# The last layer norm of a hybrid encoder layer: from three engines with a hand-set lag to VectorE and ScalarE alone

## The chip, the cores and the metric

One core of one Trainium2 chip runs the whole layer as one program. The metric is device time in microseconds (us) of that core, from runs that compute the reference's output. The engines are named as in the profile: PE is TensorE, DVE is VectorE, ACT is ScalarE, POOL is GpSimd, SP is SyncE, which here only issues transfers.

## The reference, cut to what matters

The layer takes 2048 tokens of width 1024: a projection, a gated delta rule in both directions beside attention, an output product, a first norm, a mixture of 32 experts (two per token), and a last norm. Only the end matters here:

```python
x = layer_norm(ALPHA * x + gt1 * mixed, ln1_g, ln1_b)
h = layer_norm(x) * (1.0 + sc2) + sh2
ffn = hierarchical_moe(h, ...)
x = layer_norm(ALPHA * x + gt2 * ffn, ln2_g, ln2_b)   # the last norm

def layer_norm(x, gain, bias):
    mu = mean(x); var = mean(square(x - mu))           # over the 1024 columns
    return (x - mu) * rsqrt(var + 1e-5) * gain + bias
```

## The kernel before

**Stages.** `run` (L2127) calls the stages in order: projections, attention, recurrence, output product with the first norm (`mix`), experts (`experts`, L2050) and the last norm (`tail`, L2078). Tokens are tiled in 16 tiles of 128 rows (one row per partition) by 1024 columns in 32-bit floats, 512 KB each.

**What comes before the last norm.** The scaled residual stream lies in device memory in `d_x1`. The experts work through blocks of 128 token slots and, between them, three "quads" (four small experts at once; `quads`, L1968, puts their steps at fixed places among the blocks). Each block and each quad ends with an indirect transfer issued by POOL that adds its rows into `d_x1` (L1893, L1964). The loads of the last norm read `d_x1`, so they wait for the last of these additions. Gain and bias, `g2` and `b2`, are loaded to all partitions at the end of `experts` (L2067, L2068) into tiles that held gathered tokens (they are called `xg` in the profile).

**The last norm.** `tail` first issues 16 loads from SP's queue, one tile each (L2085). Then three steps per tile are written out by hand with lags: in round t, `stats` of tile t, `scale` of tile t - 2 and `shift` of tile t - 5 (`SL`, `TL`, L2122 to L2125). Inside `manual_schedule` the engines named take their instructions in the order in which they are written.

- `stats` (L2091): for 13 tiles DVE takes the moments, two `bn_stats` of 512 columns and one `bn_aggr` (`ln_moments`, L221 and L222), and ACT takes the square root (L2101). For tiles 4, 8 and 12 (`TA`) ACT makes the moments itself: a pass whose sum goes to a column of `mv` (L2094), two small instructions that divide it (L2095, L2096), a pass that squares the centred tile and sums it (L2097), and the square root (L2098). A pass with a sum is two instructions in the profile, the pass and a read of the accumulator.
- `scale` (L2103): DVE inverts the root (L2105) and forms -mean/deviation in a column of `mv` (L2111); ACT makes the normalised tile in one pass (L2112); POOL multiplies it by `g2` (L2113). The last tile (`TP` = 1) takes another way: DVE does it in two passes, (y - mean) * g2 and y / deviation + b2 (L2107, L2108).
- `shift` (L2115): DVE adds `b2` (L2117) and ACT's queue issues the store of the tile (L2118; L2109 for the last tile).

The first norms, in `mix_norm`, use the same two DVE passes on tiles of the same size (L1330, L1333) with a reciprocal between them (L1331).

Of the kernel before, what the change touches and what calls it, by code (L numbers as in the profile page):

```python
# [13 lines left out]
AF = mybir.ActivationFunctionType  # L14
OP = mybir.AluOpType
# [4 lines left out]
D = 1024  # L20
S = 2048
NT = S // 128
# [9 lines left out]
ET = mybir.EngineType  # L32
# [14 lines left out]
FEW, QS = 32, 3  # L47
QA = (13, 18, 21, 24, 27, 30, 33, 36, 39)
QL = ((0, 1), (2, 3))
TP, SL, TL = 1, 2, 5  # L50
TA = (4, 8, 12)


def dram_ap(t, offset, ap):
# [3 lines left out]
class Layer:  # L58
# [2019 lines left out]
    def tail(self):  # L2078
        nc, tc, A = self.nc, self.tc, self.A
        with self.pool("tail", 1) as wp:  # L2080
            row = lambda t: slice(t * 128, t * 128 + 128)
            Y = [wp.tile([128, D], F32, name=f"y{t}") for t in range(NT)]
            g2, b2 = self.g2, self.b2
            for t in range(NT):
                nc.sync.dma_start(Y[t], self.d_x1[row(t)])  # L2085

            mv = [wp.tile([128, 3], F32, name=f"mv{t}") for t in range(NT)]

            sq = wp.tile([128, D], F32, name="sq")

            def stats(t):  # L2091
                y, m, act = Y[t], mv[t], nc.scalar.activation
                if t in TA:
                    act(sq, y, AF.Identity, accum_out=m[:, 2:3])  # L2094
                    act(m[:, 0:1], m[:, 2:3], AF.Identity, scale=1.0 / D)  # L2095
                    act(m[:, 2:3], m[:, 2:3], AF.Identity, scale=-1.0 / D)  # L2096
                    act(sq, y, AF.Square, bias=m[:, 2:3], accum_out=m[:, 1:2])  # L2097
                    act(m[:, 1:2], m[:, 1:2], AF.Sqrt, bias=self.eps[1e-5], scale=1.0 / D)  # L2098
                    return
                self.ln_moments(wp, y, m)  # L2100
                act(m[:, 1:2], m[:, 1:2], AF.Sqrt, bias=self.eps[1e-5])  # L2101

            def scale(t):  # L2103
                y, m = Y[t], mv[t]
                nc.vector.reciprocal(m[:, 1:2], m[:, 1:2])  # L2105
                if t >= NT - TP:
                    nc.vector.scalar_tensor_tensor(y, y, m[:, 0:1], g2, op0=OP.subtract, op1=OP.mult)  # L2107
                    nc.vector.scalar_tensor_tensor(y, y, m[:, 1:2], b2, op0=OP.mult, op1=OP.add)  # L2108
                    nc.scalar.dma_start(A["out"][0, row(t), :], y)  # L2109
                    return  # L2110
                nc.vector.scalar_tensor_tensor(m[:, 2:3], m[:, 0:1], -1.0, m[:, 1:2], op0=OP.mult, op1=OP.mult)  # L2111
                nc.scalar.activation(y, y, AF.Identity, bias=m[:, 2:3], scale=m[:, 1:2])  # L2112
                nc.gpsimd.tensor_tensor(y, y, g2, op=OP.mult)  # L2113

            def shift(t):  # L2115
                if t < NT - TP:
                    nc.vector.tensor_tensor(Y[t], Y[t], b2, op=OP.add)  # L2117
                    nc.scalar.dma_start(A["out"][0, row(t), :], Y[t])  # L2118

            with tc.manual_schedule(engines={ET.DVE, ET.Activation, ET.Pool}):  # L2120
                nc.scalar.activation(mv[0][:, 2:3], self.eps[1e-5], AF.Sqrt)
                for t in range(NT + TL):  # L2122
                    for f, lag in ((stats, 0), (scale, SL), (shift, TL)):
                        if 0 <= t - lag < NT:
                            f(t - lag)  # L2125

    def run(self):  # L2127
        tc = self.tc
# [66 lines left out]
```

## Time and profile before

| | us |
|---|---|
| median of 3 runs | 2256.69 |
| lowest and highest run | 2247.44, 2260.79 |
| the profiled execution, its own time | 2251.07 |
| its span, first to last instruction | 2249.3 |

Share of the span in which each engine is busy: PE 90%, DVE 73%, ACT 56%, POOL 39%. These are averages over all stages; the last norm takes the final 3% of the span, from the first load at 2180.1 us to the end at 2249.3 us, and PE does nothing there. Times in rows are us from the span's start, durations in the columns "mean" or "min/median/max" are ns. A row of the timeline gives start, duration, engine, line, operation, output<-input and count; a duration includes time in which the instruction was held back after it had started, and the starts of neighbours can be closer than their durations, since the end of one overlaps the beginning of the next.

### The profile page before, as it was taken

The numbers are of one execution on the slowest core, as the hardware profiler recorded it, in microseconds if no ns is written. First come the engines' busy times: TensorE is split into PE (matmuls) and PEld (weight loads), VectorE is DVE, ScalarE is ACT, GpSimd is POOL, SyncE is SP. The second block draws the span as 40 slices with busy tenths as digits, with TensorE's granted clock in tenths as the row PEclk, the third lists the DMA queues.
The fourth block names the chain that finished last, engine by engine and source line by source line (L and its number), as shares of the span: only waits on it lengthen the run. The fifth ranks groups of instructions, "written<-read, shape, count | busy, mean of one in ns | idle before, by whom it ended". The sixth has DMA issues, their size and how long they took to land. (4 is left out here: it accounts for less than half of the span.)

```text
span 2249.3 us, 43324 instructions
## 1 busy us (share of the span) xinstructions
PE 2024.6 (90%) x15381; PEld 1784.8 (79%) x15381; DVE 1650.0 (73%) x3412; ACT 1253.9 (56%) x3049; POOL 882.7 (39%) x940
## 2 busy tenths in 40 slices
PE   6999998999999999989899999999996999999940
PEld 4899997999998888878888898888775777676630
DVE  5787748288775888878787556799776877676649
ACT  4776755367754778767777444334333555454424
POOL 0311134311131447686866455402244343333227
PEclk8999999999999999999999999999997999999975
DMA  7445653445445774677752788654534999999955
GB/s 275 147 125 152 152 175 109 125 130 148 138 138 140 223 192 131 171 185 175 202 113 62 270 289 294 221 178 169 144 113 138 271 324 320 330 323 337 326 174 216
DMA packets 406939, 441.34 MB, mean 196 GB/s; under 512 B 79947, under 2 KB 331179, under 8 KB 405691
## 3 DMA queue, kind: packets, MB, share of 16 engines
q1 hardware_dynamic: 388187, 394.30, 57.1%
q0 software_dynamic: 13920, 33.71, 6.1%
q10 hardware_dynamic: 4608, 10.49, 1.2%
q8 instruction: 123, 2.02, 0.4%
q14 instruction: 101, 0.83, 0.1%
HBM read 352.15 MB, written 121.37 MB: 211 GB/s over the span
## 5 line engine op out<-in xcount | busy, mean ns | idle before, releaser
L73 PE MATMUL pj<-wh,hthi 128*128 128x256 f32 (+1 forms) x768 | 225.5, 294 | 3.1 <-DVE lnmv L222 3.1
L74 PE MATMUL pj<-wl,hthi 128*128 128x256 f32 (+1 forms) x768 | 220.0, 286 | 2.8 <-DVE wl L68 2.8
L73 PE MATMUL pj<-hthi,wh 128*128 128x260 f32 x768 | 222.5, 290 | 0.0
L75 PE MATMUL pj<-wh,htlo 128*128 128x256 f32 (+1 forms) x768 | 220.1, 287 | 1.4 <-DVE htlo L275 1.4
L207 POOL TENSOR_TENSOR xa<-xa 128x512 f32<-128x512 f32 (+2 forms) x96 | 84.2, 877 | 349.0 <-ACT xa L205 304.7
L68 DVE TENSOR_TENSOR ptl<-pt,pth 128x512 fp32r<-128x512 f32 x256 | 176.1, 688 | 58.9 <-ACT pth L67 57.6
L75 PE MATMUL pj<-hthi,wl 128*128 128x260 f32 x768 | 217.1, 283 | 0.0
L74 PE MATMUL pj<-htlo,wh 128*128 128x260 f32 x768 | 216.6, 282 | 0.0
L67 ACT CAST pth<-pt 128x512 fp32r<-128x512 f32 x256 | 150.3, 587 | 96.9 <-PE pt L884 94.0
L329 DVE SCALAR_TENSOR_TENSOR cacc<-pj,convw,cacc 128x256 f32<-128x256 f32 x384 | 183.9, 481 | 10.0
L875 ACT ACTIVATE p<-s,mx 128x512 f32<-128x512 f32 x256 | 176.9, 691 | 14.7 <-DVE mx L866 12.9
L863 DVE TENSOR_REDUCE mx<-s 128x1 f32<-128x512 f32 x256 | 175.1, 684 | 9.6 <-PE s L75 4.0
L1893 POOL DMA_INDIRECT d_x<-ye,tid x40 | 76.3, 1908 | 257.4 <-DMA d_x<-ye,tid 118.2
L73 PE MATMUL o<-pth,vh 128*128 128x256 f32 x512 | 166.0, 324 | 0.2 <-ACT oT L904 0.2
L884 PEld LDWEIGHTS pt<-ident,p 128*128 128x128 f32 x1024 | 125.3, 141 | 44.6 <-DVE ptl L68 14.2
L884 PE MATMUL pt<-ident,p 128*128 128x128 f32 x1024 | 156.2, 275 | 3.7 <-DVE ptl L68 3.3
L68 DVE TENSOR_TENSOR w13l<-raw,w13h 128x2048 fp32r<-128x2048 f32 x54 | 123.6, 2290 | 39.1 <-ACT w13h L67 38.1
L73 PEld LDWEIGHTS pj<-wh,hthi 128*128 128x128 f32 x768 | 148.1, 193 | 3.3 <-issue 3.3
L74 PEld LDWEIGHTS pj<-wl,hthi 128*128 128x128 f32 x768 | 148.0, 193 | 3.0 <-DVE wl L68 3.0
L75 PEld LDWEIGHTS pj<-wh,htlo 128*128 128x128 f32 x768 | 147.9, 193 | 2.1 <-DVE htlo L275 2.1
L75 PE MATMUL o<-pth,vl 128*128 128x256 f32 x512 | 144.9, 283 | 0.0
L74 PEld LDWEIGHTS pj<-htlo,wh 128*128 128x128 f32 x768 | 144.8, 189 | 0.0
(534 smaller groups left out, 6369.4 us busy)
## 6 DMA issues: line engine op xcount, KB each, us to landing
raw<-in_w_dram SPq DMA_DIRECT2D x116, 512.0 KB
raw<-in_w_dram SPq DMA_DIRECT2D x29, 1024.0 KB
sh<-d_sh SPq DMA_DIRECT2D x32, 768.0 KB
qraw<-in_w_dram SPq DMA_DIRECT2D x48, 512.0 KB
xa<-in_w_ada_dram SPq DMA_DIRECT2D x32, 512.0 KB
dr<-d_dir SPq DMA_DIRECT2D x32, 512.0 KB
wraw<-in_w_in_dram SPq DMA_DIRECT2D x96, 128.0 KB
qraw<-in_w_dram SPq DMA_DIRECT2D x12, 1024.0 KB
```

The lines of the kernel that those rows point to most:

```text
L67: (copy or self.nc.scalar.copy)(hi, src)
L68: (engine or self.nc.vector).tensor_tensor(lo, src, hi, op=OP.subtract)
L73: mm(out, a[0], b[0], start=start, stop=False)
L74: mm(out, a[0], b[1], start=False, stop=False)
L75: mm(out, a[1], b[0], start=False, stop=stop)
L207: nc.gpsimd.tensor_tensor(w[:, :n], w[:, :n], w[:, n:2 * n], op=OP.add)
L329: nc.vector.scalar_tensor_tensor(acc, ps[:, j:j + BLK], self.convw[:, j, ct:ct + 1], acc, op0=OP.mult, op1=OP.add)
L863: nc.vector.tensor_reduce(mx[:, i:i + 1], ps, axis=AX.X, op=OP.max)
L875: self.nc.scalar.activation(p[:, i * 512:i * 512 + 512], ps[i], AF.Exp, bias=mx[:, 4:5], scale=scale, accum_out=sm[:, i:i + 1])
L884: nc.tensor.transpose(pt[:, i, t], self.P[u, t][0][:, (2 * g + i) * 128:(2 * g + i + 1) * 128], self.ident)
L1893: self.nc.gpsimd.indirect_dma_start(out=self.d_x1, out_offset=bass.IndirectOffsetOnAxis(ap=self.tid[:, self.col(i)], axis=0), in_=self.YE. ...
```

## The change

The moments of 14 tiles are made by ACT in two summing passes (the scale of the first makes its sum the negative mean at once, so that the small divisions go); tiles 0 and 2 (`TD`) keep DVE's `bn_stats`. These two are written ahead of the loop. Every tile is then finished by DVE in the two passes that only the last tile took before. POOL has no work left in the stage, the lags are gone, and the stores are issued by SP's queue, behind the loads, instead of ACT's. Nothing else in the program is changed.

```diff
--- before.py
+++ after.py
@@ -47,8 +47,7 @@
 FEW, QS = 32, 3
 QA = (13, 18, 21, 24, 27, 30, 33, 36, 39)
 QL = ((0, 1), (2, 3))
-TP, SL, TL = 1, 2, 5
-TA = (4, 8, 12)
+TD = (0, 2)
 
 
 def dram_ap(t, offset, ap):
@@ -2085,44 +2084,32 @@
                 nc.sync.dma_start(Y[t], self.d_x1[row(t)])
 
             mv = [wp.tile([128, 3], F32, name=f"mv{t}") for t in range(NT)]
-
             sq = wp.tile([128, D], F32, name="sq")
 
-            def stats(t):
+            def moments(t):
+
                 y, m, act = Y[t], mv[t], nc.scalar.activation
-                if t in TA:
-                    act(sq, y, AF.Identity, accum_out=m[:, 2:3])
-                    act(m[:, 0:1], m[:, 2:3], AF.Identity, scale=1.0 / D)
-                    act(m[:, 2:3], m[:, 2:3], AF.Identity, scale=-1.0 / D)
-                    act(sq, y, AF.Square, bias=m[:, 2:3], accum_out=m[:, 1:2])
-                    act(m[:, 1:2], m[:, 1:2], AF.Sqrt, bias=self.eps[1e-5], scale=1.0 / D)
+                if t in TD:
+                    act(m[:, 1:2], m[:, 1:2], AF.Sqrt, bias=self.eps[1e-5])
                     return
-                self.ln_moments(wp, y, m)
-                act(m[:, 1:2], m[:, 1:2], AF.Sqrt, bias=self.eps[1e-5])
-
-            def scale(t):
+                act(sq, y, AF.Identity, scale=-1.0 / D, accum_out=m[:, 0:1])
+                act(sq, y, AF.Square, bias=m[:, 0:1], accum_out=m[:, 1:2])
+                act(m[:, 1:2], m[:, 1:2], AF.Sqrt, bias=self.eps[1e-5], scale=1.0 / D)
+
+            def finish(t):
                 y, m = Y[t], mv[t]
+                nc.vector.scalar_tensor_tensor(y, y, m[:, 0:1], g2, op0=OP.subtract if t in TD else OP.add, op1=OP.mult)
                 nc.vector.reciprocal(m[:, 1:2], m[:, 1:2])
-                if t >= NT - TP:
-                    nc.vector.scalar_tensor_tensor(y, y, m[:, 0:1], g2, op0=OP.subtract, op1=OP.mult)
-                    nc.vector.scalar_tensor_tensor(y, y, m[:, 1:2], b2, op0=OP.mult, op1=OP.add)
-                    nc.scalar.dma_start(A["out"][0, row(t), :], y)
-                    return
-                nc.vector.scalar_tensor_tensor(m[:, 2:3], m[:, 0:1], -1.0, m[:, 1:2], op0=OP.mult, op1=OP.mult)
-                nc.scalar.activation(y, y, AF.Identity, bias=m[:, 2:3], scale=m[:, 1:2])
-                nc.gpsimd.tensor_tensor(y, y, g2, op=OP.mult)
-
-            def shift(t):
-                if t < NT - TP:
-                    nc.vector.tensor_tensor(Y[t], Y[t], b2, op=OP.add)
-                    nc.scalar.dma_start(A["out"][0, row(t), :], Y[t])
-
-            with tc.manual_schedule(engines={ET.DVE, ET.Activation, ET.Pool}):
+                nc.vector.scalar_tensor_tensor(y, y, m[:, 1:2], b2, op0=OP.mult, op1=OP.add)
+                nc.sync.dma_start(A["out"][0, row(t), :], y)
+
+            with tc.manual_schedule(engines={ET.DVE, ET.Activation}):
                 nc.scalar.activation(mv[0][:, 2:3], self.eps[1e-5], AF.Sqrt)
-                for t in range(NT + TL):
-                    for f, lag in ((stats, 0), (scale, SL), (shift, TL)):
-                        if 0 <= t - lag < NT:
-                            f(t - lag)
+                for t in TD:
+                    self.ln_moments(wp, Y[t], mv[t])
+                for t in range(NT):
+                    moments(t)
+                    finish(t)
 
     def run(self):
         tc = self.tc
```

## Rows read from the trace of the kernel before

**Rows 1.** The chain of waits that ended last: start, us, what.
```profile
2180.14 3.50 DMA y<-d_x
...
2185.42 1.30 DVE lnst L221 x2
...
2186.99 1.30 DVE lnst L221 x2
...
2213.14 0.72 DVE mv L2111
2213.86 1.14 DVE y L2117
2214.99 1.21 DVE lnst L221 x2
...
2242.82 2.27 DVE y L2117 x2
```

**Rows 2.** Busy us by stretch: instructions (x), PE clock, DMA share, GB/s.
```profile
2184.00:2190.00 6.00, 0.00 (x0) 0.00 (x0) 5.66 (x14) 2.04 (x4) 0.00 (x0) 0.50 1.02 410
...
2190.20:2240.60 50.40, 0.00 (x0) 0.00 (x0) 49.58 (x70) 28.82 (x45) 47.14 (x15) 0.50 0.55 222
...
2227.10:2227.60 0.50, 0.00 (x0) 0.00 (x0) 0.50 (x2) 0.28 (x1) 0.50 (x2) 0.50 0.21 82
...
2247.00:2248.00 1.00, 0.00 (x0) 0.00 (x0) 0.00 (x0) 0.00 (x0) 0.00 (x0) 0.50 0.72 287
```

**Rows 3.** Instructions on tile y: count, duration ns min/median/max, first and last start.
```profile
L2113 POOL TENSOR_TENSOR y<-y,xg x15: 2340/3393/3399, 2190.1 to 2237.3; 128x1024 f32<-128x1024 f32 x15
L2117 DVE TENSOR_TENSOR y<-y,xg x15: 1210/1211/1212, 2196.1 to 2243.9; 128x1024 f32<-128x1024 f32 x15
...
L2107 DVE SCALAR_TENSOR_TENSOR y<-y,mv,xg x1: 3283/3283/3283, 2235.1 to 2235.1; 128x1024 f32<-128x1024 f32 x1
```

**Rows 4.** Groups of instructions, end of the span: count, busy us, mean ns, idle before.
```profile
L2111 DVE SCALAR_TENSOR_TENSOR mv<-mv 128x1 f32<-128x1 f32 x15 | 17.5, 1166 | 0.5
```

**Rows 5.** Timeline: DVE's reciprocal and the small product after it, tile 0.
```profile
2188.43 0.11 DVE L2105 RECIPROCAL mv<-mv 128x1 f32<-128x1 f32 x1
...
2188.58 0.16 DVE L2111 SCALAR_TENSOR_TENSOR mv<-mv 128x1 f32<-128x1 f32 x1
```

**Rows 6.** The first norms' DVE passes, by line, columns as in rows 3.
```profile
L1330 DVE SCALAR_TENSOR_TENSOR raw<-raw,lnmv,g x16: 1265/1284/1473, 1459.0 to 1678.5; 128x1024 f32<-128x1024 f32 x16
...
L1333 DVE SCALAR_TENSOR_TENSOR xg<-xg,lnmv,sh x16: 1272/1277/1281, 1466.1 to 1684.3; 128x1024 f32<-128x1024 f32 x16
```

**Rows 7.** Timeline: such a pass and the reciprocal behind it.
```profile
1678.54 1.27 DVE L1330 SCALAR_TENSOR_TENSOR raw<-raw,lnmv,g 128x1024 f32<-128x1024 f32 x1
1679.74 0.15 DVE L1331 RECIPROCAL lnmv<-lnmv 128x1 f32<-128x1 f32 x1
```

**Rows 8.** Timeline: ACT's own moments of tile 4.
```profile
2193.66 1.04 ACT L2094 ACTIVATE sq<-y 128x1024 f32<-128x1024 f32 x1
...
2194.82 0.20 ACT L2095 ACTIVATE mv<-mv 128x1 f32<-128x1 f32 x1
...
2195.29 1.15 ACT L2097 ACTIVATE sq<-y,mv 128x1024 f32<-128x1024 f32 x1
...
2196.56 0.29 ACT L2098 ACTIVATE mv<-mv,eps 128x1 f32<-128x1 f32 x1
2196.76 1.23 ACT L2112 ACTIVATE y<-y,mv 128x1024 f32<-128x1024 f32 x1
```

**Rows 9.** SP's queue: its loads and what they waited for (us, times, longest).
```profile
2180.14 17.34 SPq L2085 DMA_DIRECT2D y<-d_x  x16
...
SPq L2085 <- DMA y<-d_x: 10.5, 7, 2.2
```

**Rows 10.** Timeline: the issue of one store, late in the stage.
```profile
2225.10 0.34 ACTq L2118 DMA_DIRECT2D out_dram<-y  x1
```

**Rows 11.** The page's groups: a DVE operation of twice the columns.
```profile
L68 DVE TENSOR_TENSOR w13l<-raw,w13h 128x2048 fp32r<-128x2048 f32 x54 | 123.6, 2290 | 39.1 <-ACT w13h L67 38.1
```

## The prediction

> **What bounds the kernel now.** I read the chain of waits from its end, since the change touches only the last norm. From the first load at 2180.14 to the end it has no PE work: one load (3.50 us), then DVE without a break until 2245.09 (2242.82 + 2.27), then the last store [rows 1]. DVE is on the chain, but is DVE full of work? The stretch table says no more than that it never idles: 49.58 of 50.40 us, with POOL at 47.14 [rows 2]. The groups settle it. L2111 works on one column per partition, took 0.16 us before POOL had started [rows 5], and averages 1166 ns over its 15 cases [rows 4]: 17.5 us of DVE's time, of which some 15 us (15 x 1.0) are no work. POOL's multiply takes 2340 ns at its quickest and 3393 ns in the median; the difference, 1.05 us, is near the 1.21 us of DVE's addition L2117 [rows 3]. So in this trace the two engines hold each other back wherever both work on tensors or columns of this stage, and a tile costs their sum. The reader should see the rhythm in the chain: held small product 0.72, addition 1.14, `bn_stats` 1.21 [rows 1], 3.07 us, which with the aggregate and the reciprocal fill up the 3.39 us of POOL's multiply [rows 3]. The bound is POOL's multiply plus what DVE does in POOL's gaps; the loads are in by about 2203 (worked out below) and ACT has 28.82 of 50.40 us to do [rows 2].
>
> **The change part by part.** Everything is counted in the span's time, from the moment at which DVE can begin to finish tiles.
>
> *Start.* The load order and the wait before it are unchanged, so tile 0 is seen at 2183.64 [rows 1]. At 410 GB/s [rows 2] a tile of 0.524 MB takes 1.28 us, so tile 2 is there at 2186.2 and the last at 2202.8 (estimates; the trace shows that its statistics could start at 2186.99, the upper end, and 2185.42, where tile 1's started, is the lower end). One tile's statistics take 1.57 us (2185.42 to 2186.99) [rows 1]. DVE has tile 0's done before; it begins tile 0's first pass at 2186.2 + 1.57 = 2187.8, between 2187.0 and 2188.6.
>
> *DVE per tile.* Two passes of 1024 columns and a reciprocal. The operation is the one of L1330 and L1333, same shape and memory: 1284 and 1277 ns in the median [rows 6]; since ends overlap, the next instruction starts 1.20 us after (1678.54 to 1679.74) [rows 7]. The reciprocal with the instruction that needs it costs 0.15 (2188.43 to 2188.58) [rows 5]. That makes 1.20 + 0.15 + 1.20 = 2.55 us, 16 times 40.8 us. Ends: 0.07 less if the second pass started during the reciprocal, 0.05 more if each wait on ACT costs an instruction: 2.48 to 2.60, that is 39.7 to 41.6. Held at the slowest pass seen, 1.473 [rows 6], a tile would take 2.93 and all 46.9. I take 2.55, because the two medians differ by 7 ns and only one form has such an outlier.
>
> *ACT per tile.* First summing pass 1.16 (2193.66 to 2194.82, accumulator read included), second 1.27 (2195.29 to 2196.56), root 0.20 [rows 8]: 2.63 us; the two small divisions between them (0.47) go. With nothing saved it would be the whole 3.10 (2193.66 to 2196.76). ACT begins tile 1 when it has taken tile 0's root, at about 2185.7, ends it at 2188.3, takes tile 2's root and does 13 more tiles by 2188.6 + 34.2 = 2222.8. DVE wants the last tile's sums at 2187.8 + 15 x 2.55 = 2226.1. So ACT's passes are hidden, with 3.3 us to spare; it would become the bound above about 2.88 us a tile. ACT waits for DVE only at tiles 0 and 2; nothing else is queued behind those waits that could be run earlier.
>
> *What goes.* POOL's 15 multiplies, ACT's 15 normalising passes, the 15 additions, the 15 small products with their stalls, and 11 of 13 tiles' `bn_stats` on DVE. Nothing is put down to these singly: they are replaced by the new pace.
>
> *The stores.* 16 issues of 0.34 us [rows 10] move from ACT's queue to SP's, behind the loads. SP issues loads for 17.34 us, to 2197.5, because from the ninth on it waits for earlier ones to land [rows 9]. So the first three stores (ready from 2190.4) wait till 2197.5, and the load data occupies the transfers until about 2202.8. This costs nothing as long as the 16 stores, 16 x 1.28 = 20.5 us of data, can follow: 2223.3 at the earliest, ahead of DVE. If a store were put ahead of a load, that load would be late by the store's wait, but harmless while at least four tiles lie between them (landing 3.5, ACT 2.6, DVE 2.55, against 2.55 per tile).
>
> *End.* DVE's last pass ends at 2187.8 + 40.8 + 0.1 (the overlap that nothing follows) = 2228.7. A lone store issued at 2225.10 [rows 10] moves its last bytes at about 2227.2 (82 of 410 GB/s in the half microsecond from 2227.1) [rows 2], 2.1 us after. From the last bytes, 2247.7 (287 of 410 in the microsecond from 2247.0) [rows 2], to the span's end are 1.6 us. Before, four stores came within 3.4 us and queued, and the end lay 4.2 us after DVE; now 3.7, between 3.5 and 4.2. The end is 2232.4.
>
> **Sum.** 2249.3 - 2232.4 = 16.9 us less (0.75%). On the profiled execution's 2251.07 that is 2234.2. This execution stands 5.6 us below the median of the runs shown; from the median, 2239.8.
>
> **A rule that speaks against it.** In the first norms a pass of this operation over 1024 columns, all from on-chip memory, takes 1.28 us [rows 6], and an addition of as many columns takes 1.21 [rows 3], so it runs nearly at the addition's rate. The Trainium skill, Vector Engine (DVE) Microarchitecture Reference, section 7 (Points that are easy to get wrong), says that this shape of instruction has half the throughput when both its sources are in SBUF and neither is bf16. By that, DVE would be slower after the change than before (second rival); these rows disagree.
>
> **Rivals.**
>
> *First: the pass is longer here, and the gain shrinks.* DVE and ACT now stream tiles while transfers run at 410 GB/s. At 1.473 us a pass the gain is 16.9 - 6.1 = 10.8 us. For: one of 16 passes of that form took it [rows 6]. Against: the medians of both lines lie within 1%, and L1333's 16 cases between 1272 and 1281 ns. ACT as the bound belongs here: at 3.10 it ends at about 2189 + 40.3, DVE 2.5 us later at 2231.8, a gain of 13.8. Chance 0.13.
>
> *Second: half rate.* A pass then costs what twice the columns cost, 2.29 us [rows 11]; a tile takes 2 x 2.29 + 0.15 = 4.7, all 75.7, the end 2187.8 + 75.7 + 3.7 = 2267.2: 18 us slower. It decides from the point at which 16 tiles fill the time to the old end: (2249.3 - 3.7 - 2187.8) / 16 = 3.61 a tile, 1.73 us a pass. Against it stand rows 6. The page named above would have it so. Chance 0.02.
>
> *Third: the pass is slow in this stage itself.* The nearest row in place is L2107, the same pass on the same tiles, and it took 3.28 us [rows 3]. If that is not POOL's doing, a tile costs 2 x 3.28 + 0.15 = 6.7 us and the end comes at 2187.8 + 107.2 + 3.7 = 2298.7, 49 us slower; the same 1.73 decides. Against: POOL's last multiply starts at 2237.3 [rows 3], and L2107 (2235.1 + 3.28 = 2238.4) ends 1.1 us after that, so it fits a pass that waited for the multiply before it. Chance 0.03.
>
> **How the numbers follow.** The forecast has the rest, 0.82. A measurement of this kernel tells some 0.5%, 11.3 us, from no change. The shown runs alone spread over 13 us, so I let the forecast's 16.9 be measured below 11.3 in one case of eight (0.10), and half of the first rival: faster 0.72 + 0.06 = 0.78, same 0.10 + 0.07 = 0.17, slower 0.05. The bounds of the terms give a gain of 10.8 to 19.1 (best tile 1.1, best start 0.8, best end 0.2 more, with a little rounding). The lowest run less the forecast gain is 2230.5, the highest less the least gain 2250.0; the range is 2230 to 2250, and leaves out the second and third rival and a part of the first.
>
> **What would show it.** Right: L2107 and L2108 sixteen times each (under the changed kernel's numbers) at 1.27 to 1.29 us, starts of one tile's first pass 2.55 apart, DVE never idle from 2187.8 to 2228.7, ACT at 2.63 a tile and finished some 3 us ahead, no POOL work, 3.7 us from DVE's end to the span's. Wrong: DVE waiting for ACT before first passes (first rival), passes at 2.3 (second) or 3.3 (third), loads issued after stores, or a stretch before 2180 that has moved by more than a few us.

## The result, and the profile after

The changed kernel took 2237.74 us in the median of four runs (2234.89 to 2242.82), the kernel before 2256.86 in the median of its four (2247.44 to 2260.79). The ratio is 0.9921, with a 95% interval of 0.9898 to 0.9944: faster by 0.8%, and by more than 0.5% over the whole interval. The profiled execution took 2234.89 us with a span of 2233.0, 16.2 us less than the profiled execution of before (2251.07), where 16.9 were forecast.

First the instructions on tile `y`, with the columns of rows 3 (count, duration in ns as min/median/max, first and last start). L2101 and L2103 are DVE's two passes, L2095 and L2096 ACT's two summing passes, L2104 the stores, L2084 the loads:

```profile
L2084 SPq DMA_DIRECT2D y<-d_x x16: 319/325/469, 2179.6 to 2192.8; - x16
L2101 DVE SCALAR_TENSOR_TENSOR y<-y,mv,xg x16: 1276/1280/1285, 2187.5 to 2226.3; 128x1024 f32<-128x1024 f32 x16
L2103 DVE SCALAR_TENSOR_TENSOR y<-y,mv,xg x16: 1283/1285/1286, 2188.9 to 2227.7; 128x1024 f32<-128x1024 f32 x16
...
L2095 ACT ACTIVATE sq<-y x14: 1039/1040/1042, 2185.2 to 2219.7; 128x1024 f32<-128x1024 f32 x14
...
L2096 ACT ACTIVATE sq<-y,mv x14: 1147/1148/1150, 2186.4 to 2220.9; 128x1024 f32<-128x1024 f32 x14
```

All 32 DVE passes lie between 1276 and 1286 ns, where the one of L2107 took 3283 before [rows 3]. POOL has no row in the stage any more, and the 3393 ns multiply and the held product of 1166 ns [rows 3, 4] are gone with it. Next, two tiles in the timeline (start, duration, engine, line; in brackets the idle time before and what ended it):

```profile
2184.78 0.21 DVE L221 BATCH_NORM_AGGREGATE mv<-lnst 128x2 f32<-128x12 f32 x1
...
2185.90 1.29 DVE L220 BATCH_NORM_STATS2 lnst<-y 128x6 f32<-128x512 f32 x2 [0.91 <-DMA y<-d_x]
...
2187.49 1.28 DVE L2101 SCALAR_TENSOR_TENSOR y<-y,mv,xg 128x1024 f32<-128x1024 f32 x1
...
2188.70 0.16 DVE L2102 RECIPROCAL mv<-mv 128x1 f32<-128x1 f32 x1
2188.89 1.28 DVE L2103 SCALAR_TENSOR_TENSOR y<-y,mv,xg 128x1024 f32<-128x1024 f32 x1
...
2190.09 1.28 DVE L2101 SCALAR_TENSOR_TENSOR y<-y,mv,xg 128x1024 f32<-128x1024 f32 x1
...
2222.18 0.29 ACT L2097 ACTIVATE mv<-mv,eps 128x1 f32<-128x1 f32 x1
...
2227.73 1.28 DVE L2103 SCALAR_TENSOR_TENSOR y<-y,mv,xg 128x1024 f32<-128x1024 f32 x1
```

DVE stands 0.91 us for tile 2's load, begins the first pass at 2187.49, and from there each tile takes 2.59 us (the next tile's first pass starts at 2190.09; the last second pass ends at 2229.01, so 16 tiles took 41.5). ACT is done at 2222.5, 3.9 us before DVE begins the last tile at 2226.34. Last, what SP's queue waited for (us in total, times, longest), which answers to rows 9:

```profile
SPq L2104 <- DVE y L2103: 25.2, 12, 2.2
SPq L2084 <- DMA y<-d_x: 6.7, 7, 1.6
SPq L2104 <- DMA y<-d_x: 4.5, 5, 0.9
```

Twelve times a store waits for DVE, at most 2.2 us: the stores are not behind. In what follows "the stage" is the time from the first load's issue to the end of DVE's last pass: 2180.14 to 2245.09 before, 64.95 us, and 2179.56 to 2229.01 after, 49.45 us. It is the measure for small edits, for a reason that the last section shows.

### The profile page after: what moved, and what is told of

The parts are those of the page before. It is cut to its first block, busy times and chain, and to the rows that moved or that the text cites. A ratio compares the mean times of both kernels' runs of the same rounds, so it can differ in the third digit from the quotient of the medians.

```text
span 2233.0 us, 43291 instructions
## 1 busy us (share of the span) xinstructions
PE 2018.3 (90%) x15381; PEld 1783.1 (80%) x15381; DVE 1632.6 (73%) x3379; ACT 1260.4 (56%) x3072; POOL 838.5 (38%) x925
## 5 line engine op out<-in xcount | busy, mean ns | idle before, releaser
L1892 POOL DMA_INDIRECT d_x<-ye,tid x40 | 81.0, 2026 | 253.5 <-DMA d_x<-ye,tid 112.2
L73 PE MATMUL o<-ptl,vh 128*128 128x256 f32 x512 | 145.0, 283 | 0.0
```

The source lines that it names most:

```text
L73: mm(out, a[0], b[1], start=False, stop=False)
L1892: self.nc.gpsimd.indirect_dma_start(out=self.d_x1, out_offset=bass.IndirectOffsetOnAxis(ap=self.tid[:, self.col(i)], axis=0), in_=self.YE. ...
```

## The experiments

All runs in one table: the median or single time in us, that of the kernel before on the same chip, and the stage. But for the run with three rounds (six runs) they are single runs.

| run | time | before beside it | stage |
|---|---|---|---|
| 16 multiplications on POOL | 2268.39 | 2249.26 | 79.2 |
| 40 fills on POOL | 2243.02 | 2249.26 | 50.4 |
| 16 scalings on POOL | 2245.11 | 2257.46 | 58.1 |
| before, multiplication on DVE | 2287.2 | 2249.26 | 91.9 |
| before, multiplication on DVE, lagged | 2245.61 | 2252.61 | 63.2 |
| all moments on DVE | 2266.58 | 2252.61 | 70.2 |
| stores on ACT's queue | 2276.33 | 2249.26 | 90.9 |
| one tile's moments on DVE | 2244.64 | 2257.46 | 47.7 |
| reciprocal first | 2231.34 | 2252.61 | 49.1 |
| reciprocal first, tiles 0 and 1, last tile halved (3 rounds) | 2237.24 | 2252.61 | 48.4 |
| interleaved | 2239.41 | 2265.0 | 47.4 |
| interleaved, tiles 0 and 1 | 2239.76 | 2265.0 | 47.7 |

### Does POOL's multiply hold DVE, or was it the shared data?

```diff
-            with tc.manual_schedule(engines={ET.DVE, ET.Activation}):
+            with tc.manual_schedule(engines={ET.DVE, ET.Activation, ET.Pool}):
...
+                pw = wp.tile([128, D], F32, name="pw")
+                nc.gpsimd.tensor_copy(pw[:, 0:1], mv[0][:, 0:1])
+                for _ in range(16):
+                    nc.gpsimd.tensor_tensor(pw, b2, g2, op=OP.mult)
                 for t in range(NT):
                     moments(t)
                     finish(t)
```

> The changed kernel with 16 multiplications on POOL added (128x1024 f32, gain by bias into a tile of its own), none of which DVE or ACT waits for; they begin once tile 0's mean is there. Theory (POOL's two-input multiply and DVE's two-input pass hold each other back, whatever data they work on): each multiply takes about 3.4 us in place of 2.34, a DVE pass that meets one shows about 3.3 us in place of 1.28, and the stage, from the first load's issue to DVE's end, grows from 49.5 us by about 16 x 2.2 = 35 to some 84 us. Rival (in the kernel before it was the data, POOL and DVE working in turn on the same tile, that cost the time): the stage stays at 49.5 within 1 us and passes at 1.28.

The stage took 79.2 us (2183.41 to 2262.59), 29.7 more. DVE and POOL in the timeline, at the end of POOL's row of multiplications:

```profile
2227.76 13.04 POOL L2113 TENSOR_TENSOR pw<-xg,xg 128x1024 f32<-128x1024 f32 x4
2228.69 3.35 DVE L2101 SCALAR_TENSOR_TENSOR y<-y,mv,xg 128x1024 f32<-128x1024 f32 x1
2231.97 0.15 DVE L2102 RECIPROCAL mv<-mv 128x1 f32<-128x1 f32 x1
2232.16 3.17 DVE L2103 SCALAR_TENSOR_TENSOR y<-y,mv,xg 128x1024 f32<-128x1024 f32 x1
2235.25 3.35 DVE L2101 SCALAR_TENSOR_TENSOR y<-y,mv,xg 128x1024 f32<-128x1024 f32 x1
...
2238.71 3.17 DVE L2103 SCALAR_TENSOR_TENSOR y<-y,mv,xg 128x1024 f32<-128x1024 f32 x1
2241.80 1.27 DVE L2101 SCALAR_TENSOR_TENSOR y<-y,mv,xg 128x1024 f32<-128x1024 f32 x1
```

While POOL multiplies, each pass takes 3.2 to 3.4 us; the first pass after POOL's last one takes 1.27. Nothing of DVE's reads or waits for `pw`, so it is not two engines working in turn on one tile. The multiplications do read `b2` and `g2`, which DVE's passes read as well; that no common tile is needed is shown by the kernel before, where L2111 works on columns of `mv` alone and still averages 1166 ns beside POOL's multiply of `y` by `g2`, for 0.16 us without it [rows 4, 5]. Expected were 35. A tile takes 6.56 us here (L2101 starts at 2228.69 and 2235.25) for 2.59 in the changed kernel, and two multiplications go with it: 2.0 us for each, not 2.2, and the first of the 16 fell into `bn_stats`, which it did not hold. 15 x 2.0 = 30.

### Which POOL work holds it?

```diff
-                for _ in range(16):
-                    nc.gpsimd.tensor_tensor(pw, b2, g2, op=OP.mult)
+                for _ in range(40):
+                    nc.gpsimd.memset(pw, 0.0)
```

> The changed kernel with 40 fills of zeros on POOL added (128x1024 f32 into a tile of its own, about 0.95 us each by the trace of before), from the same point on. Theory of a hold by any POOL work: passes of DVE wait, the stage grows from 49.5 us by 20 us or more. Rival (only POOL work that reads its operands from SBUF holds DVE): passes stay at 1.28, the stage at 49.5 within 1 us.

By tile, the fills of this run, and then DVE's passes beside them:

```profile
L2113 POOL MEMSET pw<- x40: 950/951/952, 2192.7 to 2232.0; 128x1024 f32 x40
```

```profile
L2101 DVE SCALAR_TENSOR_TENSOR y<-y,mv,xg x16: 1277/1279/1285, 2195.7 to 2234.6; 128x1024 f32<-128x1024 f32 x16
```

The fills run beside all of DVE's passes but the last three, and neither side is held. The stage took 50.4 us, and the 0.95 more is tile 2's load, for which DVE stood 1.86 us here and 0.91 in the changed kernel:

```profile
2194.10 1.29 DVE L220 BATCH_NORM_STATS2 lnst<-y 128x6 f32<-128x512 f32 x2 [1.86 <-DMA y<-d_x]
```

So it is not any POOL work. The same place with 16 scalings that read one tensor:

```diff
-                    nc.gpsimd.tensor_tensor(pw, b2, g2, op=OP.mult)
+                    nc.gpsimd.tensor_scalar(pw, b2, 2.0, None, op0=OP.mult)
```

> The changed kernel with 16 one-input scalings on POOL added (128x1024 f32, twice the bias into a tile of its own), as in the run with 16 multiplications. Theory (POOL work that reads SBUF holds DVE's two-input passes, one input or two): DVE passes stretch and the stage grows by about 16 times the scaling's own duration less what overlaps, 15 us or more. Rival (two engines with two inputs each are needed): passes stay at 1.28 and the stage at 49.5 within 1 us.

Again by tile, the scalings and then DVE's passes:

```profile
L2113 POOL TENSOR_SCALAR pw<-xg x16: 2786/3088/3112, 2187.0 to 2234.3; 128x1024 f32<-128x1024 f32 x16
```

```profile
L2101 DVE SCALAR_TENSOR_TENSOR y<-y,mv,xg x16: 1272/1273/1285, 2189.1 to 2236.6; 128x1024 f32<-128x1024 f32 x16
L2103 DVE SCALAR_TENSOR_TENSOR y<-y,mv,xg x16: 1285/1866/1869, 2190.4 to 2238.0; 128x1024 f32<-128x1024 f32 x16
```

The stage took 58.1 us, 8.7 more: neither expectation. A tile's second pass (but for the last tile's) is 0.58 us longer (1866 for 1285), the first is untouched, though the scaling runs nearly all the time. So the one-input operation holds DVE for a small part of its duration, the two-input one for nearly all of it. Why was not tried, nor why it is the second pass that is longer. That pass reads `b2`, as the scaling does; it also starts each time some 0.6 us after a scaling has started, and the first pass over 2 us after, as here:

```profile
2193.06 3.08 POOL L2113 TENSOR_SCALAR pw<-xg 128x1024 f32<-128x1024 f32 x1
...
2193.62 1.87 DVE L2103 SCALAR_TENSOR_TENSOR y<-y,mv,xg 128x1024 f32<-128x1024 f32 x1
...
2195.41 1.27 DVE L2101 SCALAR_TENSOR_TENSOR y<-y,mv,xg 128x1024 f32<-128x1024 f32 x1
```

Whether the common tile or the moment counts, this run can't tell. The Trainium skill, SBUF — State Buffer, section "SBUF: two separate sides", says that DVE's operations with two SBUF inputs and those GpSimd operations that read SBUF exclude each other through a shared pair of ports, for a whole instruction. The multiplications and the fills agree with it; the scaling agrees that there is a hold, but it lasted 0.6 us of a 2.8 us instruction.

### POOL out, and nothing else

```diff
# in the kernel before
-                nc.gpsimd.tensor_tensor(y, y, g2, op=OP.mult)
+                nc.vector.tensor_tensor(y, y, g2, op=OP.mult)
```

> The kernel before with one word changed: the multiplication by the gain is done by DVE in place of POOL, everything else as it was. Theory (the hold alone is gone, DVE's own work stays): the small product falls from 1.17 to 0.16 us, DVE does 12 tiles of about 4.2 us, 3 of 2.65 and one of 4.2, 62.5 us from about 2184, ends near 2246, so the span is within 3 us of before's: taking POOL out gains nothing by itself, since 15 multiplications of 1.2 us come to DVE. Rival (the small product is slow for another reason): it stays at over 1 us and the span is some 15 us longer than before's.

The small product took 0.16 us, as the theory had it, and L2107, the only first pass in the form of the changed kernel, 1267 ns in place of 3283; the span was 2285.4, which the theory had not:

```profile
L2111 DVE SCALAR_TENSOR_TENSOR mv<-mv x15: 158/159/160, 2197.7 to 2271.2; 128x1 f32<-128x1 f32 x15
L2107 DVE SCALAR_TENSOR_TENSOR y<-y,mv,xg x1: 1267/1267/1267, 2275.2 to 2275.2; 128x1024 f32<-128x1024 f32 x1
```

The waits of this run (who waited for whom, us, times, longest) name the reason for the span:

```profile
ACT mv L2101 <- DVE mv L2105: 37.7, 11, 3.9
DVE y L2113 <- ACT y L2112: 27.6, 15, 4.5
```

The multiplication stands directly behind ACT's pass of the same tile. POOL could wait there while DVE went on; DVE, once it has the multiplication in its own order, stands still 15 times. The stage took 91.9 us, 27.6 of them this wait, and the hold is gone. So the question, what POOL's absence is worth by itself, was asked again with the order mended:

```diff
# in the kernel before
-                nc.gpsimd.tensor_tensor(y, y, g2, op=OP.mult)
+
+            def gain(t):
+                if t < NT - TP:
+                    nc.vector.tensor_tensor(Y[t], Y[t], g2, op=OP.mult)
...
-                    for f, lag in ((stats, 0), (scale, SL), (shift, TL)):
+                    for f, lag in ((stats, 0), (scale, SL), (gain, 4), (shift, TL)):
```

> The kernel before with the multiplication by the gain on DVE, as in the run that only changed the engine, but as a step of its own two rounds behind the normalising pass, so that DVE doesn't stand waiting for ACT. Theory (that run lost 27.6 us to DVE's waits for ACT's pass of the same tile, a matter of order): the waits go, DVE does 62.5 us of work, the stage, from the first load's issue to DVE's end, is about 66 us against 65.0 before. Rival (DVE must wait for ACT somewhere in any order): the stage stays over 80.

The stage took 63.2 us (2176.82 to 2240.01; 66 were expected), 1.8 less than before and 13.7 more than after, and DVE's waits for ACT are gone. Taking POOL out, with the moments left where they were, returns almost nothing: some 15 us of holds on the small product, and 4 on the last tile's two passes, are paid out again as 15 multiplications of 1.2 us on DVE.

### DVE's two passes, without ACT's sums

```diff
-TD = (0, 2)
+TD = tuple(range(16))
```

> The changed kernel with DVE's statistics for all 16 tiles, in front of the loop; ACT does only the roots. It leaves out the other half of the change, ACT's sums. Theory (DVE's work adds up, nothing else binds): 16 x 1.57 + 16 x 2.59 = 66.6 us from tile 0's arrival, 3.8 us after the first issue: a stage of about 70.4, 5 us longer than before's 65.0 and 21 longer than the changed kernel's 49.5. Rival (ACT's sums pace the changed kernel and don't matter to DVE): a stage under 55.

The stage took 70.2 us (2190.57 to 2260.80), as worked out: 5.3 more than before, 20.8 more than after. So without POOL, but with the moments on DVE, the stage is 1.8 us shorter (old passes) or 5.3 longer (new ones) than before; with the moments on ACT as well it is 15.5 shorter. DVE is the bound in all of them, and POOL out, by itself, does not take enough off it. The moments on ACT with POOL's multiplication left in place were not tried; that they would not be enough either is argued from the hold (29.7 us with 16 multiplications), not shown.

### Why the stores moved

```diff
-                nc.sync.dma_start(A["out"][0, row(t), :], y)
+                nc.scalar.dma_start(A["out"][0, row(t), :], y)
```

> The changed kernel with its stores issued by ACT's queue again, at the same place in the program. Theory (an engine's instructions wait in order, so the store of tile t, which waits for DVE, holds up ACT's sums of tile t+1): ACT and DVE take turns, a tile of ACT's costs 2.4 + 2.6 + 0.2 = about 5.2 us, and the stage grows from 49.5 us by some 36, to 85. Rival (a transfer's wait doesn't hold the engine's later work): no change within 1 us.

One tile of this run in the timeline:

```profile
2201.63 1.28 DVE L2101 SCALAR_TENSOR_TENSOR y<-y,mv,xg 128x1024 f32<-128x1024 f32 x1 [2.87 <-ACT sq L2096]
...
2204.34 0.34 ACTq L2104 DMA_DIRECT2D out_dram<-y  x1
2204.73 1.06 ACT L2095 ACTIVATE sq<-y 128x1024 f32<-128x1024 f32 x1 [2.80 <-DVE y L2103]
...
2207.18 1.28 DVE L2101 SCALAR_TENSOR_TENSOR y<-y,mv,xg 128x1024 f32<-128x1024 f32 x1 [2.87 <-ACT sq L2096]
```

DVE and ACT take turns: 5.55 us a tile (2201.63 to 2207.18), each standing 2.8 for the other. The stage took 90.9 us, 41.5 more; expected were 36, without the issue of 0.34 us, which lies on the path too. In the kernel before, where the store is written five rounds behind, the same queue did no harm: no wait of ACT's there is put down to the addition L2117 that a store follows. In the changed kernel, with the lags gone, the move to SP is no side matter.

### How near is ACT?

```diff
-TD = (0, 2)
+TD = (0,)
```

> The changed kernel with DVE's statistics for tile 0 alone: ACT makes the sums of 15 tiles. Theory (DVE at 2.59 and ACT at 2.64 us a tile are nearly even, and DVE begins 2.5 us earlier): DVE now waits a little for ACT at nearly every tile, ACT ends its last sums about 45 us after the first load's issue and DVE 2.6 us later, a stage of 47.6 us. Rival (ACT has room to spare): a stage of 49.5 - 2.5 = 47.0 with DVE never waiting.

The stage took 47.65 us (2191.20 to 2238.85), as worked out, and 1.8 less than the changed kernel's: DVE began its passes 5.8 us after the first load's issue in place of 7.9. From the end of the timeline, three first passes of DVE and ACT's root before the last one:

```profile
2230.89 1.28 DVE L2101 SCALAR_TENSOR_TENSOR y<-y,mv,xg 128x1024 f32<-128x1024 f32 x1
...
2233.53 1.28 DVE L2101 SCALAR_TENSOR_TENSOR y<-y,mv,xg 128x1024 f32<-128x1024 f32 x1
...
2236.17 0.29 ACT L2097 ACTIVATE mv<-mv,eps 128x1 f32<-128x1 f32 x1
2236.17 1.28 DVE L2101 SCALAR_TENSOR_TENSOR y<-y,mv,xg 128x1024 f32<-128x1024 f32 x1
```

First passes are now 2.64 us apart, ACT's pace, and the last starts when ACT's last sum is there. The two engines are that even: one tile more on ACT and it sets the pace. The stage is shorter even so, nearly as much as by the best of the three attempts that follow, and with one constant changed.

### Three attempts to go further

The first puts the reciprocal ahead of the passes:

```diff
+                nc.vector.reciprocal(m[:, 1:2], m[:, 1:2])
                 nc.vector.scalar_tensor_tensor(y, y, m[:, 0:1], g2, op0=OP.subtract if t in TD else OP.add, op1=OP.mult)
-                nc.vector.reciprocal(m[:, 1:2], m[:, 1:2])
```

> The changed kernel with each tile's reciprocal ahead of its first pass in place of between the passes. Theory (the second pass waits 0.19 us for the reciprocal that it directly follows; with a pass between them the reciprocal costs some 0.07): 16 x 0.12 = 1.9 us off the stage, 49.5 to 47.5, a tile 2.47 us. Rival (the reciprocal must then wait for ACT's root, or DVE's order doesn't matter): a stage of 49.5.

The stage took 49.1 us (2176.34 to 2225.46), 0.3 less: a miss. In DVE's timeline a tile reads:

```profile
2199.69 1.26 DVE L2102 SCALAR_TENSOR_TENSOR y<-y,mv,xg 128x1024 f32<-128x1024 f32 x1
2200.99 1.28 DVE L2103 SCALAR_TENSOR_TENSOR y<-y,mv,xg 128x1024 f32<-128x1024 f32 x1
2202.19 0.15 DVE L2101 RECIPROCAL mv<-mv 128x1 f32<-128x1 f32 x1
2202.26 1.27 DVE L2102 SCALAR_TENSOR_TENSOR y<-y,mv,xg 128x1024 f32<-128x1024 f32 x1
```

The reciprocal now costs 0.07 (2202.19 to 2202.26), as expected, but the second pass starts 1.30 after the first in place of 1.20: it reads what the first writes, and where another tile's pass stands between them (the third attempt) starts lie 1.18 to 1.20 apart again. What the reciprocal had cost it had also hidden. The second attempt had this edit, tiles 0 and 1 on DVE's statistics, and the last tile's second pass and store in two halves:

```diff
-TD = (0, 2)
+TD = (0, 1)
...
-                nc.vector.scalar_tensor_tensor(y, y, m[:, 1:2], b2, op0=OP.mult, op1=OP.add)
-                nc.sync.dma_start(A["out"][0, row(t), :], y)
+                for s in [slice(0, D)] if t < NT - 1 else [slice(0, 512), slice(512, D)]:
+                    nc.vector.scalar_tensor_tensor(y[:, s], y[:, s], m[:, 1:2], b2[:, s], op0=OP.mult, op1=OP.add)
+                    nc.sync.dma_start(A["out"][0, row(t), s], y[:, s])
```

> The changed kernel with three small edits: the reciprocal ahead of the first pass (1.9 us), tiles 0 and 1 in place of 0 and 2 with DVE's statistics (0.9: DVE stood for tile 2's load), and the last tile's second pass and store in two halves (the last store is half as long, 0.6 us). Theory (DVE alone sets the pace): a stage of 46.6 to 46.8 us and 3.4 us in place of 4.0 from DVE's end to the span's, 3.4 us less in all, 0.15% of the time: less than runs can tell, so it is read from the trace. Rival (ACT is close behind and binds when DVE is quicker): a stage of 48 or more, with DVE waiting for ACT.

The stage took 48.4 us (2179.25 to 2227.62), and from there to the span's end 3.9, not 3.4: the 0.9 for tile 2's load came, the reciprocal's did not, and the halves gained nothing (a second half pass costs 0.13, and the span's end came only 0.1 sooner behind a half store than behind a whole one). 48.4 lies where the rival had put it, but not for its reason: no pass of DVE's waits for ACT in this run. The two halves:

```profile
2226.21 1.41 DVE L2104 SCALAR_TENSOR_TENSOR y<-y,mv,xg 128x512 f32<-128x512 f32 x2
```

In runs the ratio to before was 0.9926 (0.9892 to 0.996), which cannot be told from the changed kernel's. The third attempt put another tile's pass between the two of one tile; `first` is the first pass and the reciprocal of `finish`, `second` its second pass and store:

```diff
-                for t in range(NT):
-                    moments(t)
-                    finish(t)
+                for t in range(NT + 1):
+                    if t < NT:
+                        moments(t)
+                        first(t)
+                    if t:
+                        second(t - 1)
```

> The changed kernel with the second pass of a tile put behind the first pass of the next tile. Theory (in the run with the reciprocal in front, the second pass started 1.30 us after the first instead of 1.20, since it reads what the first writes; so the gap goes only if another tile's pass stands between): tiles 1.20 + 0.07 + 1.20 = 2.47 us apart instead of 2.59, a stage of 49.5 - 1.9 = 47.6 us. Rival (0.1 us is lost at every second pass whatever stands before it, or ACT binds): 49 or more.

The stage took 47.4 us (2186.09 to 2233.52), and DVE's timeline shows passes 1.18 to 1.20 apart, 2.45 a tile:

```profile
2206.47 0.15 DVE L2102 RECIPROCAL mv<-mv 128x1 f32<-128x1 f32 x1
2206.54 1.26 DVE L2106 SCALAR_TENSOR_TENSOR y<-y,mv,xg 128x1024 f32<-128x1024 f32 x1
2207.72 1.28 DVE L2101 SCALAR_TENSOR_TENSOR y<-y,mv,xg 128x1024 f32<-128x1024 f32 x1
2208.92 0.15 DVE L2102 RECIPROCAL mv<-mv 128x1 f32<-128x1 f32 x1
```

With tiles 0 and 1 in place of 0 and 2 on top of it:

```diff
-TD = (0, 2)
+TD = (0, 1)
```

> The same with tiles 0 and 1 on DVE's statistics in place of 0 and 2. Theory (DVE no longer stands for tile 2's load, 0.8 to 0.9 us in the runs so far, and ACT keeps ahead): a stage of 46.7 us. Rival (ACT, 2.63 us a tile from tile 2 on, begins to bind a DVE at 2.47): DVE waits for ACT and the stage stays at 47.5.

Here the rival held: 47.7 us (2186.13 to 2233.79). Counted from the first load's issue, DVE began 1.2 us earlier, but ACT had to wait for tile 1's statistics before its first sums and started them 1.6 us later. Towards the end it paced DVE, whose first passes start with ACT's roots, 2.64 us apart:

```profile
2227.41 0.29 ACT L2097 ACTIVATE mv<-mv,eps 128x1 f32<-128x1 f32 x1
2227.41 1.28 DVE L2101 SCALAR_TENSOR_TENSOR y<-y,mv,xg 128x1024 f32<-128x1024 f32 x1
...
2230.05 0.29 ACT L2097 ACTIVATE mv<-mv,eps 128x1 f32<-128x1 f32 x1
2230.05 1.28 DVE L2101 SCALAR_TENSOR_TENSOR y<-y,mv,xg 128x1024 f32<-128x1024 f32 x1
```

The three arrangements with the shortest stages (tile 0 alone, and the two interleaved ones) lie between 47.4 and 47.7 us, paced by one engine or the other; less was not reached. The interleaved form is 2 us better than the changed kernel in the stage, 0.09% of the time; its one run, 2239.41 beside 2265.0 of the kernel before, can't show that.

## Why the prediction was right

*The bound.* "[T]he two engines hold each other back wherever both work on tensors or columns of this stage" was the step everything hung on, and the run with multiplications on a tile of their own shows it: passes of 3.2 to 3.4 us beside POOL, 1.27 without. The third rival, a pass that is slow in this stage itself, falls with the same row, and with the multiplication moved to DVE in the kernel before: L2107 took 1267 ns there, so its 3.28 us were POOL's doing. "On tensors or columns" was too wide: fills on POOL hold nothing, a one-input scaling holds a fifth of its time.

*Half rate.* The second rival is out: 32 passes of two float inputs from SBUF at 1276 to 1286 ns, 0.56 of the 2290 ns that twice the columns cost [rows 11]. The rule of the Trainium skill that was weighed in the prediction, from Vector Engine (DVE) Microarchitecture Reference, section 7, does not hold for this form here.

*The terms.* Start: tile 0's first pass was forecast 7.7 us after the first load's issue (2187.8 - 2180.1) and came 7.9 after. Tile: 2.55 forecast, 2.59 measured. The pass was right at 1.20; the reciprocal with what follows cost 0.19 for the 0.15 that two one-column instructions had shown [rows 5]. A second pass right behind its first starts 1.30 after it even without a reciprocal between, so 0.10 of the 0.19 is the second pass's dependence on the first, a term that the prediction did not have. ACT: 2.63 forecast, 2.64 measured, 3.9 us ahead at the end for the 3.3 forecast, and in two runs, with one tile fewer on DVE (2.59 us a tile) and interleaved with tiles 0 and 1 (2.45), ACT at 2.64 sets the pace, so "hidden" was right with little room. End: 3.7 forecast, 4.0 measured: 2.2 from DVE's end to the last bytes (2.1 forecast), 1.8 from there to the end (1.6). Together the stage and its end are 1.2 us longer than forecast; the loads of this execution were issued 0.6 us earlier. Sum: 2233.0 for 2232.4.

That the two ends lie so close is in part luck. The first load was issued at 2176.3 to 2191.2 in the traces of the experiments, a spread nearly as large as the gain, and the prediction held it fixed at 2180.1; it happened to move by only 0.6 us between these two executions. What the prediction foresaw is the stage: by its terms 48.6 us (2228.7 - 2180.1) from 64.95, measured 49.45.

*What goes and what stays.* The first rival, longer passes beside transfers, did not come: no pass over 1286 ns while loads and stores ran. The stores on SP's queue cost nothing, as forecast, and on ACT's they would have cost 41.5 us. The loads took SP 13.6 us, not the 17.3 of rows 9, so that the first store was issued at 2194.2 and not at 2197.5; nothing hung on it.

*The median.* 2239.8 forecast, 2237.74 measured. Of the medians' 19.1 us the stage explains 15.5 and the end behind it 0.2; the rest is within what the runs spread.

## What to carry to other kernels

An engine that is busy all the time may be held rather than working: compare the duration of its smallest instruction with the same instruction where the other engine is idle, and look there for a partner whose own duration grows by the same amount. When work is moved off such a pair, count what it adds to the engine that stays: here putting POOL's multiplication on DVE was worth 1.8 us by itself, and the whole change, with the moments moved to ACT as well, 15.5. A store or a multiplication that waits for another engine belongs behind a lag or on a queue with nothing behind it; written directly behind its producer it made two engines take turns.

## What the runs showed that was not expected

Two DVE passes of which the second reads the first's output start 1.30 us apart, two independent ones 1.18 to 1.20 (both 128x1024); the reciprocal between a dependent pair adds 0.1 (1.40, 2187.49 to 2188.89 above). POOL's scaling of one tensor holds DVE's two-input pass for 0.58 us of its 2.8 to 3.1, its fill of 0.95 us not at all, its two-tensor multiply for some 2.0 of 2.35.

And the part of the program that no edit touched moves more than most edits do. The first norms' first pass (by line, columns as above), in the changed kernel and in the run with fills on POOL:

```profile
L1329 DVE SCALAR_TENSOR_TENSOR raw<-raw,lnmv,g x16: 1269/1284/1287, 1457.3 to 1676.0; 128x1024 f32<-128x1024 f32 x16
```

```profile
L1329 DVE SCALAR_TENSOR_TENSOR raw<-raw,lnmv,g x16: 1275/1284/1503, 1468.3 to 1688.9; 128x1024 f32<-128x1024 f32 x16
```

Its first start lies 11 us apart, and the last norm's first load was issued between 2176.3 and 2191.2 in the traces of the experiments. What makes it so was not looked into. For that reason edits of a few us are told here by the stage, whose instructions take the same from trace to trace (only tile 2's load lands up to 0.95 us later or earlier), and not by the time of a run.
